# Low halves of the delta branch's chunk matrices: subtraction on GpSimd instead of VectorE

## The chip, the cores and the metric

The kernel is one program on one core of a Trainium2 chip. The metric is the device time of that core in microseconds (us). A core has five engines that run their own instruction queues in order and meet through semaphores: TensorE (PE, matmuls into PSUM), VectorE (DVE), ScalarE (ACT), GpSimd (POOL, which cannot read PSUM) and SyncE (SP, here a queue that only issues DMAs). POOL issues DMAs too.

## What is computed

One inference step of a hybrid backbone for two groups of tokens, 2048 sample tokens and 128 context tokens, with a model width of 1024. After an adaptive RMSNorm, one input projection feeds three branches of width 512, and a gated sum of the branches goes through an output projection:

```python
    proj = jnp.einsum('btd,de->bte', xn, w_in)
    ...
    o_f, s_f = gated_delta_chunked(q, k, v, g[:, :, 0], beta[:, :, 0], s0_f)
    ...
    o_b = chunk_sgu(u_b, v_b, sgu_norm_g, w_spatial, b_spatial) * jax.nn.silu(z_b)
    o_c = fourier_mix(x_c, grid) * jax.nn.silu(z_c)
    ...
    merged = jnp.einsum('btnd,btnd->btd', gt, pb)
    return jnp.einsum('btd,de->bte', merged, w_out), s_f, s_b
```

The change lies in branch A, the gated delta rule, which is run forwards and backwards over the sequence (`dec_strict` and `dec_incl` are masks of decays):

```python
    m = eye + bc[..., :, None] * jnp.einsum('bnhik,bnhjk->bnhij', kc, kc) * dec_strict
    sol = lax.linalg.triangular_solve(m, rhs, left_side=True, lower=True, unit_diagonal=True)
    ...
    qk = jnp.einsum('bnhik,bnhjk->bnhij', qc, kc) * dec_incl
```

## The kernel before

Numbers that need more than 16 bits are kept as a pair of fp16 tiles: the high half is the value rounded to fp16, the low half is what the rounding left. A product of two pairs is three matmuls (`mm3`, L163). Powers of two (`FS` is 4096) bring the values into the range of fp16.

The program is a long stream of matrix products: the normalised tokens (L438 to L469), the q, k, v columns with their short convolution (L606 to L631), branch B (L1155 to L1200), branch C (from L1213) and the merge and output projection. Branch A is cut in 17 chunks of 128 tokens with 4 heads. Its small, dependent steps are written as a Python generator, `delta()` (L1067), and laid between the large products: `pace.tick` (L320), called after each product with an amount of time, moves the generator to its next `yield` for each `QUOTA` of 1.6. So the program order around the change is that of the ticks. The framework then orders each engine's queue by that priority and by a timing model of its own, with the parts under `high_priority` first; what comes out is one fixed order for each engine.

`delta()` runs `prep` (L673) for each chunk and, interleaved with it, `base_inverse` (L758) for the group of chunks before. The groups are chunk 16 alone and then four of four chunks. A scan over all chunks and both directions follows (L917).

`prep` of one chunk, in eight steps:

- transposes of k, v and q on PE (`turned`, L682), squares on ACT (L688), a small addition on DVE (L689) and the power -1/2 on POOL (L690), and the scaled k in `tok` on DVE (L699);
- q split in a pair (L708, L709); `tok` is stored from POOL's queue (L711), transposed on PE (L715) and split into the pair `T` (L716 on ACT, L717 on DVE);
- the product of keys with keys in a PSUM bank (L726). For each direction: four DVE instructions (L731) multiply it by beta and the decays into the fp32 tile `n_` (names n32, three buffers), four ACT copies (L733) take its diagonal blocks into `nd`, ACT makes the high half (L735) and DVE the low half (L736) of `n16` (three buffers), and `late` (L666) queues its store on SP, which is issued at the next call of `late`;
- POOL issues two DMAs of `nd` (L740), from which `base_inverse` starts: its DVE copy L772 waits for them;
- the product of keys with queries (L743). For each direction DVE multiplies it by the decays (L746), ACT makes the high half (L748), DVE the low half (L749), and the store is queued.

The PSUM banks of `prep` come from three pools in turn. In the trace the tiles `n_`, `n16` and `p16` all appear as `n`, `tok` as `tok`, the banks as `b`.

`base_inverse` inverts the 32x32 diagonal blocks, one column after another, by pairs of DVE instructions on SBUF tiles (L779, L780), and splits the result (L785 on ACT, L786 on DVE).

Also on these engines in that stretch: the conversion of weights into pairs (`converting`, L198: ACT L209 and L218, DVE L183 to L187 and L219), and branch B's and C's gate units: ACT L1109 and DVE L1111 evict a bank, POOL multiplies (L1121), ACT squares (L1122), POOL issues the store (L1123).

`beta` carries a factor of 1/FS² through `prep` (L512), which cancels that of the pair products, and is multiplied by FS before the scan (L1092).

Of the kernel before, what the change touches and what calls it, by code (L numbers as in the profile page):

```python
# [14 lines left out]
AF = mybir.ActivationFunctionType  # L15
ALU = mybir.AluOpType
# [21 lines left out]
FS = 4096.0  # L38
# [73 lines left out]
def hybrid_flow_kernel(ctx: ExitStack, tc: tile.TileContext, x_prompt, x_sample, state_delta, c, c_ctx, ln_g, w_ada,  # L112
# [3 lines left out]
    V, A, G, PE, SY = nc.vector, nc.scalar, nc.gpsimd, nc.tensor, nc.sync  # L116
# [9 lines left out]
    def sb(pl, shape, tag, dt=F32, bufs=None):  # L126
        kw = {} if bufs is None else {"bufs": bufs}
        return pl.tile(list(shape), dt, tag=tag, name=nm(tag), **kw)
# [11 lines left out]
    def bank(pl, shape, tag="b"):  # L140
        if pl is ps_d:
            rot[0] += 1
            pl = ps_d[rot[0] % 3]
        return pl.tile(list(shape), F32, tag=tag, name=nm(tag))
# [247 lines left out]
    for blk in range(8):  # L392
# [3 lines left out]
        ps = bank(ps_d, [2, 256])  # L396
# [41 lines left out]
    for ti, (t0, tn) in enumerate(TBS):  # L438
# [13 lines left out]
        for k in range(KT):  # L452
            ps = bank(ps_d, [P, tn])
# [6 lines left out]
        for g in range(4):  # L460
            ps = bank(ps_d if tn == P and g % 2 else ps_mm, [P, tn])
# [12 lines left out]
    def h3(ap):  # L474
        return ap.rearrange("p (h x) -> p h x", h=H)
# [5 lines left out]
    beta, eg, egl, ed, neg = [sb(dp, dsh, n_) for n_ in ("beta", "eg", "egl", "ed", "neg")]  # L481
# [13 lines left out]
    def decays():  # L495
# [13 lines left out]
        pbv = pbs.rearrange("p c (s d h) -> p s d c h", s=2, d=2)  # L509
        for d in range(2):  # L510
            A.activation(beta[:, d], pbv[:, 0, d], AF.Sigmoid, scale=bdw.inv)
        V.tensor_scalar(beta, beta, 1.0 / (FS * FS), None, ALU.mult)  # L512
        yield 1
        NH = 2 * NCH * H
        blob = sb(dq, [P, 2, WB], "tok").rearrange("p d x -> p (d x)")
# [90 lines left out]
    for ct in range(12):  # L606
        w = getw(1, 2 if ct < 6 else min(4, 15 - ct))
        for half in range(1):
# [4 lines left out]
            for t0, tn in TBS:  # L613
                flip[0] ^= 1
                ps = bank(ps_d if flip[0] else ps_mm, [P, tn])
# [50 lines left out]
    def late(dst, src):  # L666

        if owed:
            SY.dma_start(*owed.pop())
        if dst is not None:  # L670
            owed.append((dst, src))

    def prep(g, ci, t, nxt, held):  # L673
# [5 lines left out]
        def turned(part):  # L679
            ps = bank(ps_d, [P, WB])  # L680
            for h in range(H):
                PE.transpose(ps[:, hs(h)], cur[part][:, h, :], ident)  # L682
            return ps
# [13 lines left out]
        ps = turned(1)  # L697
# [15 lines left out]
        ps = bank(ps_d, [P, WB])  # L713
# [8 lines left out]
        dc = cur["dc"]  # L722
        ps = bank(ps_d, [P, WB])
# [3 lines left out]
        nd = sb(d2, [P, 2, H, 32], "nd", bufs=2)  # L727
        for d in range(2):
            n_ = sb(d2, [P, WB], "n32", bufs=3)
            for h in range(H):  # L730
                V.scalar_tensor_tensor(n_[:, hs(h)], ps[:, hs(h)], beta[:, d, t, h:h + 1], dc[:, d, hs(h)], ALU.mult, ALU.mult)  # L731
            for B in range(4):
                A.copy(nd[32 * B:32 * B + 32, d], h3(n_)[32 * B:32 * B + 32, :, 32 * B:32 * B + 32])  # L733
            n16 = sb(d2, [P, 2, WB], "n16", F16, bufs=3)
            A.activation(n16[:, 0, :], n_, AF.Copy, scale=FS)  # L735
            V.scalar_tensor_tensor(n16[:, 1, :], n_, FS, n16[:, 0, :], ALU.mult, ALU.subtract)  # L736
            late(nD[d][t], n16)
            yield 1
        for d in range(2):
            G.dma_start(ndD[g][d, ci].rearrange("h p i -> p h i"), nd[:, d])  # L740
        ps = bank(ps_d, [P, WB])
        for h in range(H):
            mm3(ps[:, hs(h)], pair(T, h), pair(Q16, h))  # L743
        for d in range(2):
            q_ = sb(d2, [P, WB], "n32", bufs=3)
            V.tensor_mul(q_, ps, dc[:, d, :])  # L746
            p16 = sb(d2, [P, 2, WB], "n16", F16, bufs=3)
            A.activation(p16[:, 0, :], q_, AF.Copy, scale=1.0 / FS)  # L748
            V.scalar_tensor_tensor(p16[:, 1, :], q_, 1.0 / FS, p16[:, 0, :], ALU.mult, ALU.subtract)  # L749
            late(qkD[d][t], p16)  # L750
            yield 1

# [314 lines left out]
    def delta():  # L1067
        nonlocal dq
        seq = [(g, ci, t) for g, ts in enumerate(GROUPS) for ci, t in enumerate(ts)]
        held = {1: rows(1, 16), 2: rows(2, 16), 0: rows(0, 16), "dc": decay_rows(16)}  # L1070
        yield from bounds()
        base = iter(())
        for i_, (g, ci, t) in enumerate(seq):
            if ci == 0 and g:
                for r_ in base:
                    if r_:
                        yield 1
                base = base_inverse(g - 1)
            for n_, _ in enumerate(prep(g, ci, t, seq[i_ + 1][2] if i_ < 16 else None, held)):
                yield 1  # L1080
                if next(base, 0):
                    yield 1
        late(None, None)
        for r_ in base:
            if r_:
                yield 1
        for _ in base_inverse(4):
            yield 1
        dl.close()
        dq = pool(dl, "dqb", 1, side="right")  # L1090
        V.tensor_scalar(rq, rq, bnds[:, 2:3], None, ALU.mult)
        V.tensor_scalar(beta, beta, FS, None, ALU.mult)  # L1092
        for d in range(2):
            V.tensor_tensor(eg[:, d], eg[:, d], rq, ALU.mult)
        pace.quota, pace.fine = SCAN, True
        yield from scan()
        dl.close()
        dps.close()
# [35 lines left out]
    ps = bank(ps_x, [P, 4, P])  # L1134
# [20 lines left out]
    for t in range(NCH):  # L1155
        ps = bank(ps_mm, [P, 4, P])
# [30 lines left out]
    for g in range(4):  # L1187
# [5 lines left out]
        for ti, (t0, tn) in enumerate(TBS):  # L1193
            st = vrow[:, t0:t0 + tn]
            ps = bank(ps_mm, [P, tn])
# [17 lines left out]
    for g in range(4):  # L1213
        xw, zw = getw(2, 2)
        for gh in range(1):
# [18 lines left out]
            for q in range(0, NCH, 4):  # L1234
                qn = min(4, NCH - q)
                ps = bank(ps_mm, [P, qn, P])
# [44 lines left out]
            for q4 in range(5):  # L1281
# [8 lines left out]
                if q4 == 2:  # L1290
                    ps = bank(ps_x, [P, P])
# [180 lines left out]
    for i_, t in enumerate(order):  # L1472
# [7 lines left out]
        for i in range(2):  # L1480
            cs = slice(i * 512, (i + 1) * 512)
            ps = bank(ps_mm, [P, 512])
# [45 lines left out]
```

## Time and profile before

| | |
|---|---|
| runs | 2203.88, 2207.9 and 2209.03 us, median 2207.9 us |
| the profiled execution, its own time | 2208.47 us |
| its span, first to last instruction | 2206.7 us |
| mean granted TensorE clock | 0.994 of full speed |
| VectorE busy over the span | 1299.4 us (59%) |
| GpSimd busy over the span | 708.8 us (32%) |
| HBM traffic | 362 MB, 164 GB/s over the span |

All numbers come from one profiled execution. Busy time counts arithmetic and, for the DMA rows of POOL and SP, the issue of a DMA. A group row names the line, the engine, the operation and the tiles (out<-in) with their partitions and elements, then the count, busy us and mean ns, and after the last bar the time for which the engine stood idle in front of these instructions, with what ended it. "issue" means that the profile shows nothing that was waited for. `(+n forms)` says that other sizes are in the same row.

### The profile page before, as it was taken

The page shows a single profiled execution, that of the slowest core. Times are in us where ns is not written, and L with a number is a line of the kernel's source. Part 1 is how long each engine was busy: PE and PEld are TensorE (multiplying, and loading weights), DVE is VectorE, ACT ScalarE, POOL GpSimd, SP SyncE. Part 2 cuts the span into 40 slices and gives each one's busy share as a digit, 9 for nine tenths or more (in the row PEclk, how much of TensorE's full clock was granted, in tenths as well). Part 3 has the DMA queues.
Part 4 walks back from the last instruction along what each step waited for, and adds up shares of the span by engine and source line. Part 5 has one row for each costly group of instructions (what it writes and reads, how often), then busy time and mean ns, then how long its engine had stood idle before and what let it go on. Part 6 is the DMA issues. An engine that isn't in the chain of part 4 may idle for free.

```text
span 2206.7 us, 42033 instructions
## 1 busy us (share of the span) xinstructions
PE 2138.4 (97%) x15966; PEld 1230.7 (56%) x15966; DVE 1299.4 (59%) x3081; ACT 1005.0 (46%) x2322; POOL 708.8 (32%) x860
## 2 busy tenths in 40 slices
PE   7999999999999999899899999899999999999998
PEld 3564444455555588778555565555555444444443
DVE  5736854479869688255665555755574544233454
ACT  3545644455465564344644445655553422222332
POOL 1421333223334322432322223354442222112543
PEclk9999999999999999999999999999999999999999
DMA  8434733277686762433655556766664544333542
GB/s 280 144 94 157 277 98 101 66 214 224 219 245 221 204 187 86 118 116 119 214 178 162 171 158 187 239 185 213 201 204 150 168 124 129 118 101 120 174 149 104
DMA packets 304276, 365.05 MB, mean 165 GB/s; under 512 B 39393, under 2 KB 215626, under 8 KB 302026
## 3 DMA queue, kind: packets, MB, share of 16 engines
q1 hardware_dynamic: 288938, 302.19, 45.3%
q0 software_dynamic: 12688, 51.27, 6.5%
q10 hardware_dynamic: 2448, 8.91, 1.0%
q8 instruction: 125, 2.05, 0.4%
q14 instruction: 77, 0.63, 0.1%
HBM read 234.67 MB, written 127.62 MB: 164 GB/s over the span
## 4 chain that ended last, share of the span: by engine, by line
PE 50%; DMA 6%; DVE 5%; ACT 3%; issue 2%; POOL 1%; SPq 0%; DVEq 0%; POOLq 0%; ACTq 0%
PE b L161 49%; DMA st<-br 1%; DMA wst<-in_w_branch_dram 1%; DVE XB L779 1%; DVE E L780 1%; DMA wst<-in_w_in_dram 1%; DMA XB<-nd 0%; DMA mt<-mrg 0%; ACT of L1032 0%; POOL o L1029 0%; DVE big L1322 0%; DMA mrow<-mrg 0%; DVE wlo L219 0%; ACT big L1321 0%; DMA S<-in_state_delta_dram 0%
## 5 line engine op out<-in xcount | busy, mean ns | idle before, releaser
L161 PE MATMUL b<-xh,whi 128*128 128x512 f16 (+1 forms) x1920 | 651.3, 348 | 4.8 <-DVE vrow L1198 1.7
L161 PE MATMUL b<-xl,whi 128*128 128x512 f16 (+1 forms) x1920 | 652.1, 348 | 0.0
L161 PE MATMUL b<-xh,wlo 128*128 128x512 f16 (+1 forms) x1920 | 651.1, 348 | 0.0
L161 PEld LDWEIGHTS <-whi 128*128 128x128 f16 x3904 | 356.5, 98 | 332.9 <-issue 12.9
L161 PEld LDWEIGHTS <-wlo 128*128 128x128 f16 x1952 | 191.2, 98 | 178.4 <-issue 2.1
L161 PE MATMUL b<-big,bhi 128*128 128x512 f16 (+1 forms) x960 | 250.7, 348 | 1.0 <-DVE big L1322 1.0
L1361 POOL TENSOR_TENSOR mrow<-mrow,sg 128x512 f32<-128x512 f32 (+1 forms) x80 | 94.3, 1179 | 292.9 <-DVE sg L1360 163.8
L161 PE MATMUL b<-big,blo 128*128 128x512 f16 (+1 forms) x480 | 163.3, 347 | 0.0
L1351 ACT ACTIVATE sg<-b,winv 128x512 f32<-128x512 f32 (+1 forms) x120 | 74.1, 618 | 152.2 <-PE b L161 151.8
L161 PEld LDWEIGHTS <-xh 128*128 128x128 f16 x1496 | 117.1, 98 | 29.7 <-issue 1.4
L628 POOL TENSOR_TENSOR cy<-cy,raw 128x545 f32<-128x545 f32 (+1 forms) x48 | 69.8, 1480 | 185.9 <-ACT raw L627 185.9
L161 PEld LDWEIGHTS <-bhi 128*128 128x128 f16 x960 | 87.0, 98 | 75.8 <-issue 0.3
L175 DVE CAST wscb<-wss 128x1 bf16<-128x1 f32 x93 | 14.3, 154 | 186.1 <-ACT wlo L209 84.1
L1360 DVE SCALAR_TENSOR_TENSOR sg<-b,binv,sg 128x512 f32<-128x512 f32 (+1 forms) x80 | 53.5, 668 | 104.5 <-PE b L161 91.3
L848 POOL COPY T<-ES 32x256 f16<-32x256 f16 x68 | 29.4, 432 | 223.0 <-DMA ES<-ei 204.9
L161 PE MATMUL b<-wohi,mh 128*128 128x512 f16 x240 | 91.0, 379 | 2.6 <-ACT mh L1428 2.6
L161 PE MATMUL b<-whi,xl 128*128 128x128 f16 x544 | 92.9, 219 | 0.0
L161 PE MATMUL b<-wlo,xh 128*128 128x128 f16 x544 | 92.9, 219 | 0.0
L161 PE MATMUL b<-whi,xh 128*128 128x128 f16 x544 | 92.9, 219 | 0.0
L219 DVE SCALAR_TENSOR_TENSOR wlo<-wst,wsc,whi 128x1024 f16<-128x1024 f32 x52 | 74.4, 1434 | 28.5 <-ACT whi L218 28.2
L161 PE MATMUL b<-wohi,ml 128*128 128x512 f16 x240 | 90.9, 379 | 0.3 <-DVE mscb L175 0.3
L161 PE MATMUL b<-wolo,mh 128*128 128x512 f16 x240 | 91.0, 379 | 0.0
(449 smaller groups left out, 4283.1 us busy)
## 6 DMA issues: line engine op xcount, KB each, us to landing
wst<-in_w_in_dram SPq DMA_DIRECT2D x60, 512.0 KB, 5.4
qkv<-cy POOLq DMA_DIRECT2D x12, 1089.0 KB, 5.2
st<-br SPq DMA_DIRECT2D x48, 256.0 KB, 5.1
mrow<-mrg SPq DMA_DIRECT2D x18, 512.0 KB, 4.1
mrow<-mrg SPq DMA_DIRECT2D x16, 576.0 KB, 4.4
mrg<-mrow POOLq DMA_DIRECT2D x16, 576.0 KB, 3.6
dc<-dec SPq DMA_DIRECT2D x17, 512.0 KB, 5.2
kq<-qkv SPq DMA_DIRECT2D x34, 256.0 KB, 5.5
```

The costliest lines, as they stand in the source:

```text
L161: PE.matmul(out, l, r, start=start, stop=stop)
L175: V.tensor_copy(sb16, ss)
L219: V.scalar_tensor_tensor(w.lo, st, s, w.hi, ALU.mult, ALU.subtract)
L628: G.tensor_tensor(y[:, c0:c1], y[:, c0:c1], raw[:, 1 + c0:1 + c1], ALU.mult)
L779: V.tensor_tensor(t3, X3[:, 0:k, k:k + 1].to_broadcast([P, k, n_]), E3[:, k:k + 1, k:32].to_broadcast([P, k, n_]), ALU.mult)
L780: V.tensor_tensor(E3[:, 0:k, k:32], E3[:, 0:k, k:32], t3, ALU.subtract)
L848: G.tensor_copy(T16[rows(a0, b), :, :, b], ES[0:32, :, 2 * a0 + b, :, wT])
L1351: A.activation(sg, ps, AF.Sigmoid, scale=gw.inv)
L1360: V.scalar_tensor_tensor(sg, ps, binv[:, 1:2], sg, ALU.mult, ALU.mult)
L1361: G.tensor_tensor(mr, mr, sg, ALU.add)
```

## The change

In `prep`, both low halves (L736, L749) become plain subtractions on GpSimd, fp32 tile minus its fp16 high half. For that the fp32 tile must already have the scale of the pair. For the key product, `beta` now has a factor of 1/FS instead of 1/FS², and the diagonal blocks are divided by FS as they are copied. For the query product, the multiplication by the decays takes 1/FS with it. The high halves become plain copies on ScalarE. The factor that `beta` got before the scan (L1092) goes.

```diff
-        V.tensor_scalar(beta, beta, 1.0 / (FS * FS), None, ALU.mult)
+        V.tensor_scalar(beta, beta, 1.0 / FS, None, ALU.mult)
...
-                A.copy(nd[32 * B:32 * B + 32, d], h3(n_)[32 * B:32 * B + 32, :, 32 * B:32 * B + 32])
+                A.activation(nd[32 * B:32 * B + 32, d], h3(n_)[32 * B:32 * B + 32, :, 32 * B:32 * B + 32], AF.Copy, scale=1.0 / FS)
             n16 = sb(d2, [P, 2, WB], "n16", F16, bufs=3)
-            A.activation(n16[:, 0, :], n_, AF.Copy, scale=FS)
-            V.scalar_tensor_tensor(n16[:, 1, :], n_, FS, n16[:, 0, :], ALU.mult, ALU.subtract)
+            A.copy(n16[:, 0, :], n_)
+            G.tensor_tensor(n16[:, 1, :], n_, n16[:, 0, :], ALU.subtract)
             late(nD[d][t], n16)
...
-            V.tensor_mul(q_, ps, dc[:, d, :])
+            V.scalar_tensor_tensor(q_, ps, 1.0 / FS, dc[:, d, :], ALU.mult, ALU.mult)
             p16 = sb(d2, [P, 2, WB], "n16", F16, bufs=3)
-            A.activation(p16[:, 0, :], q_, AF.Copy, scale=1.0 / FS)
-            V.scalar_tensor_tensor(p16[:, 1, :], q_, 1.0 / FS, p16[:, 0, :], ALU.mult, ALU.subtract)
+            A.copy(p16[:, 0, :], q_)
+            G.tensor_tensor(p16[:, 1, :], q_, p16[:, 0, :], ALU.subtract)
             late(qkD[d][t], p16)
...
-        V.tensor_scalar(beta, beta, FS, None, ALU.mult)
```

## The prediction

> **What bounds the kernel now.** I read the page's first lines first, then the busy time of the stage in which the change lies, then TensorE's waits there, then the groups of VectorE, GpSimd and ScalarE.
>
> ```profile
> span 2206.7 us, 42033 instructions
> PE 2138.4 (97%) x15966; PEld 1230.7 (56%) x15966; DVE 1299.4 (59%) x3081; ACT 1005.0 (46%) x2322; POOL 708.8 (32%) x860
> ```
>
> TensorE (PE) is busy for 97% of the span. No edit here takes a matmul away, so the change can only move the idle time of PE: 68 us in all. The chunk preparation runs from about 440 us to 890 us. The row of the windows view for that stretch gives, after its bounds and length, the busy us (and instructions) of PE, PE's weight loads, VectorE (DVE), ScalarE (ACT) and GpSimd (POOL), then the granted clock.
>
> ```profile
> 440.00:890.00 450.00, 435.33 (x3356) 277.89 (x3355) 365.31 (x957) 242.80 (x722) 142.29 (x180) 0.99 0.66 199
> ```
>
> PE is idle for 14.7 us in these 450, and that is the whole gain that the stage has to give. DVE, at 81%, is the fullest engine beside PE; POOL stands at 32%. The waits of PE in the same stretch (line that waited, what it waited for: us in total, times, longest) say whose the idle time is:
>
> ```profile
> PE b L715 <- DVE tok L699: 2.9, 2, 2.2
> PE b L682 <- issue: 2.6, 1, 2.6
> PE b L161 <- ACT T L716: 2.6, 2, 2.4
> PE b L161 <- DVE vrow L1198: 1.7, 1, 1.7
> PE b L161 <- DVE wsc L185: 1.5, 1, 1.5
> PE b L161 <- DVE T L717: 1.1, 3, 0.4
> PE b L682 <- DVE n L731: 0.8, 2, 0.4
> ```
>
> No wait is long. A dozen small ones make up the sum, each where an instruction of the preparation stands at the head of PE's queue and its input is not there yet.
>
> **The change part by part.** The two subtractions leave DVE. Their groups in the stretch, with neighbours that are needed below (columns: count, busy us, mean ns, idle before and its cause):
>
> ```profile
> L779 DVE TENSOR_TENSOR XB<-XB,E 128x31 f32<-128x31 f32 (+15 forms) x155 | 57.2, 369 | 2.9
> L780 DVE TENSOR_TENSOR E<-E,XB 128x31 f32<-128x31 f32 (+15 forms) x155 | 52.9, 341 | 3.0
> ...
> L749 DVE SCALAR_TENSOR_TENSOR n<-n,n 128x512 f16<-128x512 f32 x34 | 24.5, 726 | 6.9 <-ACT n L748 6.8
> L736 DVE SCALAR_TENSOR_TENSOR n<-n,n 128x512 f16<-128x512 f32 x34 | 23.4, 689 | 7.9 <-ACT n L735 7.8
> L746 DVE TENSOR_TENSOR n<-b,dc 128x512 f32<-128x512 f32 x34 | 22.7, 685 | 1.4 <-PE b L161 1.4
> ...
> L689 DVE TENSOR_SCALAR ss<-ss 128x4 f32<-128x4 f32 x34 | 8.7, 255 | 1.1 <-ACT sq L688 1.0
> ...
> L772 DVE COPY XB<-XB 64x1024 f32<-64x1024 f32 x5 | 5.3, 1059 | 13.4 <-DMA XB<-nd 13.4
> ```
>
> *Removed from DVE:* 24.5 + 23.4 = 47.9 us of work, and 6.8 + 7.8 = 14.6 us in which DVE's queue stood still for ACT's high half: 62.5 us. Where it shows on PE is seen once, at 609.5 us, in the timelines of DVE and PE (start, us, instruction):
>
> ```profile
> 607.26 0.69 DVE L736 SCALAR_TENSOR_TENSOR n<-n,n 128x512 f16<-128x512 f32 x1 [0.28 <-ACT n L735]
> ...
> 608.12 0.69 DVE L749 SCALAR_TENSOR_TENSOR n<-n,n 128x512 f16<-128x512 f32 x1
> 608.73 0.69 DVE L746 TENSOR_TENSOR n<-b,dc 128x512 f32<-128x512 f32 x1
> ```
>
> ```profile
> 609.51 0.66 PE L682 MATMUL b<-cst,qr 128*128 128x128 f32 x4 [2.65 <-issue]
> ```
>
> PE's transposes need a bank that L746 still reads. Ahead of L746 stood one L736, its wait and one L749: 1.7 us. This wait (2.6), those on T L717 (1.1) and n L731 (0.8), and by my choice half of that on tok (1.45) are in reach of a shorter DVE queue: **6.0 us**. Not in reach are T L716 (ACT), vrow (DVE had been waiting for a DMA) and wsc L185 (DVE stood at L772).
>
> *Added to POOL:* 68 subtractions of a 128x512 tile. The same operation stands elsewhere in the program (min/median/max ns):
>
> ```profile
> L957 POOL TENSOR_TENSOR kn<-skn,kn x34: 1145/1157/1663, 903.8 to 1648.7; 128x512 f16<-128x512 f32 x34
> ```
>
> 68 x 1.157 = 78.7 us, so POOL goes from 142 to 221 us of 450: room enough in sum. But POOL is no free neighbour of DVE, as 758 us shows:
>
> ```profile
> 758.82 1.26 POOL L1121 TENSOR_TENSOR st<-sg,vrow 128x512 f32<-128x512 f32 x1 [11.65 <-DVE sg L1111]
> 760.05 1.04 POOL L690 TENSOR_TENSOR ss<-ss,mhalf 128x4 f32<-128x4 f32 x1
> ```
>
> ```profile
> 758.89 1.27 DVE L779 TENSOR_TENSOR XB<-XB,E 128x60 f32<-128x60 f32 x1
> 760.20 0.22 DVE L780 TENSOR_TENSOR E<-E,XB 128x60 f32<-128x60 f32 x1
> 760.46 0.25 DVE L779 TENSOR_TENSOR XB<-XB,E 128x87 f32<-128x87 f32 x1
> ```
>
> A 60-column L779 takes 1.27 us where its twin L780 of the same size takes 0.22: it ends when POOL's 512-column product ends. Under L690, which reads four columns, L779 has its usual length. So a wide POOL instruction holds back a DVE instruction that reads two SBUF tiles. PE waited soon after:
>
> ```profile
> 762.69 0.63 PE L715 MATMUL b<-cst,tok 128*128 128x128 f32 x4 [2.19 <-DVE tok L699]
> ```
>
> How much of it there is now follows from the groups above, the spread of L689 (min/median/max ns) and the wide POOL instructions of the stretch:
>
> ```profile
> L689 DVE TENSOR_SCALAR ss<-ss x34: 155/167/1261, 455.4 to 829.1; 128x4 f32<-128x4 f32 x34
> ```
>
> ```profile
> L1121 POOL TENSOR_TENSOR st<-sg,vrow 128x512 f32<-128x512 f32 (+1 forms) x20 | 23.0, 1151 | 66.6 <-DVE sg L1111 59.8 <-DVE vrow L1198 3.2 <-DVE winv L216 2.0
> ...
> L1121 POOL TENSOR_TENSOR st<-sg,yT 128x512 f32<-128x512 f32 (+1 forms) x5 | 5.5, 1115 | 2.3 <-DVE yT L1274 1.4 <-DVE n L749 0.6 <-DMA br<-st 0.3
> ```
>
> Against what the instructions take undisturbed, L779 lost (over L780, the same shapes) 57.2 - 52.9 = 4.3 us; L749 (over L736) 24.5 - 23.4 = 1.1; L689, with a mean of 255 ns against a median of 167, 34 x 0.088 = 3.0: together 8.4 us. L1121 took 23.0 + 5.5 = 28.5 us, so 8.4 / 28.5 = 0.29 us of DVE is lost for each us of it. The subtractions would cost 78.7 x 0.29 = 23 us (bounds: nothing, and all 78.7). I take 23, which is made of the nearest rows.
>
> The Trainium skill states the reason in "SBUF — State Buffer", section "Who interferes with whom": a VectorE instruction with two SBUF inputs contends with a GpSimd instruction that reads SBUF, and the one that comes second is blocked to the end of the other. The 1.27 us above agree. By that rule at its full length, each of the 68 subtractions with a two-input instruction behind it, all 78.7 us come back on DVE, more than the 62.5 that leave it; this is the third rival below.
>
> Net on DVE: 62.5 - 23 = 39.5 us, 63% of what is removed. Of the 6.0 us of PE in reach I take 63%: **3.8 us gained**.
>
> *ACT.* High halves lose their scale, the nd copies gain one:
>
> ```profile
> L733 ACT COPY nd<-n 32x128 f32<-32x128 f32 x136 | 39.8, 293 | 23.5 <-DVE n L731 22.3
> ...
> L748 ACT ACTIVATE n<-n 128x512 f16<-128x512 f32 x34 | 21.0, 622 | 14.0 <-DMA n<-n 11.5 <-DVE n L749 0.9 <-ACT q L708 0.8
> ```
>
> ```profile
> L956 ACT CAST kn<-skn x34: 600/618/620, 901.7 to 1647.8; 128x512 f16<-128x512 f32 x34
> ```
>
> Scaled 622, plain 618: 4 ns, times 136 copies and 68 halves, under 1 us either way, hidden since ACT is busy 243 of 450 us. ACT also waits 11.5 us for stores of n16 (three buffers). The store now follows a subtraction that is 1.157 - 0.689 = 0.47 longer; 34 times that is 16 us of ACT at most, which I cost at nothing in ACT's idle 207 us; if that cover failed it would be part of the second rival. SP's stores wait the same 0.47 at its queue's head, one step after the data is made; weights are read two ahead. L746 becomes a scaled form: 685 against the 689 of L736, no change. The beta line that goes is a single small instruction.
>
> *New waits on POOL's queue.* Each subtraction waits at the head of the queue for ACT's high half. Behind it stand the DMAs of nd (L740), the power L690, L1121 and the store of kv. Two of them matter.
>
> The second DMA of nd comes after the second subtraction in the program: ACT's conversion (0.62) and the subtraction (1.16) go ahead of it, 1.8 us. DVE's copy L772 waits at its queue's head for that data, 13.4 us over 5 groups, behind which PE lost the 1.5 us of wsc L185. 5 x 1.8 = 9 us more, at 1.5 / 13.4, is **1.0 us lost** (bounds: nothing if the DMA is put first; 9 us if PE loses every one).
>
> L690 releases tok L699, which releases PE's L715. Its slack is small. Around 494 us:
>
> ```profile
> 493.13 1.36 POOL L690 TENSOR_TENSOR ss<-ss,mhalf 128x4 f32<-128x4 f32 x1
> ```
>
> ```profile
> 495.02 0.69 DVE L749 SCALAR_TENSOR_TENSOR n<-n,n 128x512 f16<-128x512 f32 x1
> 495.63 0.69 DVE L746 TENSOR_TENSOR n<-b,dc 128x512 f32<-128x512 f32 x1
> 496.23 0.68 DVE L699 TENSOR_TENSOR tok<-b,ss 128x512 f32<-128x512 f32 x1
> ```
>
> The power is done at 494.49, tok starts at 496.23: 1.7 us in DVE's queue, of which 0.69 is an L749 that goes. A subtraction ahead of L690 makes it 1.16 later, which this slack covers. I take one full subtraction over all 17 chunks: **1.2 us lost** (bounds: nothing, and 17 x 1.16 = 19.7).
>
> **Sum:** -3.8 + 1.0 + 1.2 = -1.6 us. The profiled execution took 2208.47 us, 1.8 more than its span, and 0.6 more than the median of the runs (2207.9). 2208.5 - 1.6 = 2206.9; I forecast **2207**, no difference within 0.3% (6.6 us), which is about what a measurement of this kernel can tell from no change.
>
> **The rivals.** *First, the relief is whole (0.30).* DVE's blocking falls into its own idle time, all 6.0 us in reach go, and the other 1.45 of tok. Then the stall at the scan's start shrinks too (PE's waits from 890 to 1000 us):
>
> ```profile
> PE b L161 <- DVE X L1257: 4.2, 1, 4.2
> ```
>
> DVE stands there behind the scan's first loads, which follow the last base inverse; the last chunk's two L749 (0.7 each) before that inverse are gone, 1.4 us. 6.0 + 1.45 + 1.4 = 8.9: 2200, and 2194 if vrow, wsc and T L716 go as well. For it: DVE's 81%. Against it: the 1.27 us above.
>
> *Second, POOL's in-order queue (0.28), the case on the other side.* L690 stands behind a subtraction that itself waits for ACT, in most chunks, and PE's L715 pays. It decides once 9 or more of the 17 chunks pay a full 1.16: 10.4 - 3.8 + 1.0 = +7.6, 2216; all 17 give +16.9, 2225. I name 2219. For it: PE already waits there (2.9 us). Against it: the slack at 494.
>
> *Third, blocking at full length (0.08).* DVE gets back 78.7 - 62.5 = 16 us more than it lost, so nothing of the 6.0 is gained. PE's 2.2 us at L715 followed the block at 758, 2.2 of 8.4: 16 x 0.26 = 4.2, and 1.0 + 1.2: +6.4, 2215, on the bound.
>
> That the change does not do what it says leaves no case of its own: 68 instructions do change engine; only POOL's reading could be stretched instead of DVE's, which is the second rival.
>
> **How the numbers follow.** Forecast 0.34, rivals 0.30, 0.28 and 0.08. The third is halved over the bound: faster 0.30, same 0.38, slower 0.32. The forecast's own range is 2202 to 2213. For 8 in 10 the range takes in all of the first rival down to 2194 and the second up to 2222, with the rest outside.
>
> **What would show it.** Right: DVE's busy time in this stretch falls by 25 to 45 us, L779's mean rises above L780's by more than the 28 ns of now, POOL rises by 80 us or more, PE's wait for issue before L682 goes, and PE's idle time in the stretch stays within 5 us of 14.7. Wrong: PE's waits on tok L699 grow past 8 us (second rival), DVE's busy time does not fall (third), or PE's idle time falls under 8 us (first). If the time moves by more than the idle time of this stretch does, the order of the scan behind it has changed, which nothing here prices.

## The result, and the profile after

The changed kernel takes 2236.2 us (median of four runs, 2234.1 to 2239.4) against 2205.9 us (2203.1 to 2209.0) for the kernel before, run beside it. The ratio is 1.0138, with a 95% interval of 1.0118 to 1.0159: **1.4% slower, 30 us**, where no difference was forecast. The profiled execution took 2239.4 us and its span is 2237.7, which is 31.0 more than before. These are the first lines of its page:

```profile
span 2237.7 us, 42044 instructions
PE 2147.5 (96%) x15966; PEld 1236.2 (55%) x15966; DVE 1304.6 (58%) x3012; ACT 1007.0 (45%) x2322; POOL 784.8 (35%) x928
```

PE runs the same 15966 matmuls. It was idle for 2206.7 - 2138.4 = 68.3 us and is now idle for 2237.7 - 2147.5 = 90.2 us: 21.9 of the 31.0 are idle time. The other 9.1 are busy time: the same matmuls took longer, at a lower clock (see the end). POOL gained its 68 instructions. **DVE, which has 69 instructions fewer (the 68 and the scaling of `beta`), is busy for 5 us more than before.** That one number says that something went wrong on DVE and not only on POOL.

In the row of the chunk preparation (440 to 890 us, columns as in the prediction):

```profile
440.00:890.00 450.00, 419.06 (x3209) 267.37 (x3207) 354.91 (x843) 236.43 (x707) 215.38 (x248) 0.98 0.64 196
```

PE is idle for 30.9 us of the 450, against 14.7. DVE's 843 instructions take 354.9 us (421 ns each); before, 957 took 365.3 (382 ns). They are fewer by more than 69 because the preparation now reaches further beyond 890 us. The last high half of a query product starts at 867.4 us on ACT, before at 844.5: 22.9 of the 31 us are lost by there. The first matmul of the output projection comes 30.0 later than before (2051.2 against 2021.2), so some 7 more go in the scan and the merge, and 1 at the end.

PE's longest waits in the same stretch:

```profile
PE b L682 <- issue: 11.2, 6, 4.9
PE b L715 <- DVE tok L699: 6.1, 5, 2.7
PE b L161 <- DVE sg L1172: 4.5, 4, 2.6
PE b L161 <- DVE T L717: 4.3, 4, 1.9
```

The wait for issue before L682, which the shorter queue should have removed, went from 2.6 to 11.2 us. T L717 went from 1.1 to 4.3, tok from 2.9 to 6.1, and sg L1172 is new. All are instructions of DVE. Its groups (440 to 920 us, so that the stretch holds as many instructions as the prediction's rows do) say what happened to it:

```profile
L780 DVE TENSOR_TENSOR E<-E,XB 128x31 f32<-128x31 f32 (+15 forms) x155 | 72.9, 470 | 3.5
L779 DVE TENSOR_TENSOR XB<-XB,E 128x31 f32<-128x31 f32 (+15 forms) x155 | 65.2, 421 | 3.0
...
L709 DVE SCALAR_TENSOR_TENSOR q<-qr,qsc,q 128x512 f16<-128x512 f32 x17 | 19.7, 1158 | 3.3 <-ACT q L708 3.1
...
L689 DVE TENSOR_SCALAR ss<-ss 128x4 f32<-128x4 f32 x34 | 14.9, 437 | 8.2 <-ACT sq L688 8.2
...
L1172 DVE TENSOR_SCALAR sg<-sg,vss 128x512 f32<-128x512 f32 x17 | 10.9, 641 | 2.5 <-POOL vss L171 2.1
...
L772 DVE COPY XB<-XB 64x1024 f32<-64x1024 f32 x5 | 6.3, 1266 | 10.9 <-DMA XB<-nd 10.9
```

Two of these groups were not shown of the kernel before:

```profile
L709 DVE SCALAR_TENSOR_TENSOR q<-qr,qsc,q 128x512 f16<-128x512 f32 x17 | 12.7, 746 | 3.1 <-ACT q L708 3.1
...
L1173 DVE TENSOR_SCALAR sg<-sg,vss 128x512 f32<-128x512 f32 x17 | 8.2, 485 | 2.1 <-POOL vss L171 2.0
```

The same instructions, as many of them, on the same shapes, take longer: L780 +20.0 us, L779 +8.0, L709 +7.0, L689 +6.2, the scaling of `sg` +2.7, L772 +1.0. That is 44.9 us come back of the 47.9 removed. All of them read SBUF only. L689, the scaling of `sg` and L772, 9.9 us of the sum, read one wide tile from SBUF and not two. (L216, L219 and L786, 0.9 us each, are left out here and below.) A count over single instructions agrees: from 440 to 940 us DVE's instructions take 61.0 us more than the fast tenth of their like in these runs, against 14.2 before, and 46.0 of the 61.0 fall on instructions whose longest overlap on POOL is with a subtraction. L731, L746, L699 and L717, which read a PSUM bank, have kept their durations (L746 683 ns, before 685).

How such a microsecond reaches PE is seen at 617 us, in the timelines of DVE, POOL and PE:

```profile
617.51 0.25 DVE L780 TENSOR_TENSOR E<-E,XB 128x87 f32<-128x87 f32 x1
617.80 2.67 DVE L779 TENSOR_TENSOR XB<-XB,E 128x60 f32<-128x60 f32 x1
620.40 0.68 DVE L746 SCALAR_TENSOR_TENSOR n<-b,dc 128x512 f32<-128x512 f32 x1
621.00 0.20 DVE L780 TENSOR_TENSOR E<-E,XB 128x60 f32<-128x60 f32 x1
```

```profile
617.32 0.77 POOL L740 DMA_DIRECT2D nd<-nd  x1
618.12 1.16 POOL L736 TENSOR_TENSOR n<-n,n 128x512 f16<-128x512 f32 x1
619.23 1.16 POOL L749 TENSOR_TENSOR n<-n,n 128x512 f16<-128x512 f32 x1
```

```profile
621.18 0.72 PE L682 MATMUL b<-cst,qr 128*128 128x128 f32 x4 [4.94 <-issue]
```

A 60-column L779 takes 2.67 us where its twin L780 takes 0.20. Two subtractions run one behind the other on POOL, from 618.12 to 620.39, and L779 ends just after the second. (Why it wasn't done by 618.0, before the first, the trace doesn't say; POOL was issuing a DMA then.) L746 stands behind it in DVE's queue and frees the bank that PE's transposes want: PE stands for 4.94 us. This is the prediction's own stall at 609 us over again, with a held L779 where an L749 used to stand, and nearly twice as long.

### The profile page after: what moved, and what is told of

It reads as the page before. It is cut to its first block, busy times and chain, and to the rows that moved or that the text cites. A ratio compares the mean times of both kernels' runs of the same rounds, so it can differ in the third digit from the quotient of the medians.

```text
span 2237.7 us, 42044 instructions
## 1 busy us (share of the span) xinstructions
PE 2147.5 (96%) x15966; PEld 1236.2 (55%) x15966; DVE 1304.6 (58%) x3012; ACT 1007.0 (45%) x2322; POOL 784.8 (35%) x928
## 4 chain that ended last, share of the span: by engine, by line
PE 48%; DVE 10%; DMA 8%; ACT 3%; issue 3%; POOL 1%; SPq 1%; DVEq 0%; POOLq 0%; ACTq 0%
PE b L161 47%; DVE E L780 2%; DVE XB L779 2%; DMA st<-br 2%; DMA wst<-in_w_in_dram 1%; DMA mrg<-mrow 1%; DVE wlo L219 1%; DMA XB<-nd 1%; DMA wst<-in_w_branch_dram 1%; DMA ES<-ei 1%; DVE big L1321 1%; DVE n L731 0%; DMA br<-o 0%; DVE q L709 0%; ACT of L1032 0%
## 5 line engine op out<-in xcount | busy, mean ns | idle before, releaser
L628 POOL TENSOR_TENSOR cy<-cy,raw 128x545 f32<-128x545 f32 (+1 forms) x48 | 74.3, 1575 | 184.3 <-ACT raw L627 184.3
L1359 DVE SCALAR_TENSOR_TENSOR sg<-b,binv,sg 128x512 f32<-128x512 f32 (+1 forms) x80 | 53.5, 668 | 106.0 <-PE b L161 90.2
L219 DVE SCALAR_TENSOR_TENSOR wlo<-wst,wsc,whi 128x1024 f16<-128x1024 f32 x52 | 75.3, 1451 | 31.9 <-ACT whi L218 31.7
```

The costliest lines, as they stand in the source:

```text
L219: V.scalar_tensor_tensor(w.lo, st, s, w.hi, ALU.mult, ALU.subtract)
L628: G.tensor_tensor(y[:, c0:c1], y[:, c0:c1], raw[:, 1 + c0:1 + c1], ALU.mult)
L1359: V.scalar_tensor_tensor(sg, ps, binv[:, 1:2], sg, ALU.mult, ALU.mult)
```

## The experiments

Three theories were put against each other. **Theory 1, the port:** a wide POOL instruction that reads SBUF holds DVE instructions that read two tiles from SBUF (the 9.9 us on one-tile instructions lie outside it). **Theory 2, POOL's queue:** the instructions behind the subtractions on POOL (DMAs, the power L690) come too late. **Theory 3, the order:** the edit gave the framework other costs and it laid all queues out anew; the loss is an accident of that order. The order is never held fixed: compared in the traces by the names of the tiles, 913 of PE's 15966 matmuls stand at another place in the changed kernel than in the kernel before, and 436 to 1818 in those variants below that have as many matmuls. Ratios are those to the kernel before, run on the same chip.

### The same edit with the subtractions left on VectorE

Against the changed kernel:

```diff
-            G.tensor_tensor(n16[:, 1, :], n_, n16[:, 0, :], ALU.subtract)
+            V.tensor_tensor(n16[:, 1, :], n_, n16[:, 0, :], ALU.subtract)
...
-            G.tensor_tensor(p16[:, 1, :], q_, p16[:, 0, :], ALU.subtract)
+            V.tensor_tensor(p16[:, 1, :], q_, p16[:, 0, :], ALU.subtract)
```

> The scales are moved as in the change, but both low halves stay on VectorE, as plain subtractions of two SBUF tiles. Theory 1 (SBUF reading: a wide GpSimd subtraction holds back VectorE instructions with two SBUF inputs) and theory 2 (GpSimd's in-order queue: the power behind tok and the nd DMAs stand behind the subtractions) both expect the time of before, 2200 to 2213 us, and L779 and L780 at before's 369 and 341 ns. Theory 3 (the fixed order that the framework writes out came out worse, whatever engine subtracts) expects it clearly slower, 2220 us or more, since the edit reorders the queues too.

2209.3 us, ratio 1.0008 (0.9997 to 1.0019). The row of the preparation:

```profile
440.00:890.00 450.00, 434.68 (x3364) 279.67 (x3363) 365.27 (x956) 244.11 (x722) 142.35 (x180) 1.00 0.67 199
```

It is that of the kernel before to within 1 us on PE, DVE and POOL. The moved scale, on ACT and in `beta`, costs nothing; the loss comes with the engine of the subtraction. Of the variants this one's order is the nearest to that of before (436 matmuls elsewhere), so it says little on theory 3.

### One subtraction at a time

The key product's low half alone on POOL, the query product's on DVE:

```diff
-            G.tensor_tensor(p16[:, 1, :], q_, p16[:, 0, :], ALU.subtract)
+            V.tensor_tensor(p16[:, 1, :], q_, p16[:, 0, :], ALU.subtract)
```

> The change with only the key product's low half on GpSimd; the query product's stays on VectorE as a plain subtraction. Half of the wide reads: theory 1 expects about half of the VectorE time that is held (some 24 of 48 us) and half of the loss, 2214 to 2228 us. Theory 2 expects nearly the whole loss, since this subtraction is the one ahead of the nd DMAs: 2226 us or more. Theory 3 gives no number but no order either.

And the other way round:

```diff
-            G.tensor_tensor(n16[:, 1, :], n_, n16[:, 0, :], ALU.subtract)
+            V.tensor_tensor(n16[:, 1, :], n_, n16[:, 0, :], ALU.subtract)
```

> The change with only the query product's low half on GpSimd, the key's on VectorE as a plain subtraction: the other half of the wide reads, and none of them ahead of the nd DMAs. Theory 1 (SBUF reading) expects what the key half alone showed, held VectorE time about 24 us and 2214 to 2228 us, so that the two halves add up to about the 30 us of the change. Theory 2 (GpSimd's queue) expects before's time within 0.3%, since the nd DMAs do not wait for it.

The key product's alone costs 0.57% (0.38 to 0.76; 2220.2 us), the query product's alone 0.47% (0.31 to 0.63; 2216.8 us). Together that is 1.04 of the 1.38%: each edit has its share, and the second costs more beside the first. VectorE's groups of the two kernels, the first with the key product's on POOL:

```profile
L780 DVE TENSOR_TENSOR E<-E,XB 128x31 f32<-128x31 f32 (+15 forms) x155 | 62.4, 403 | 3.1
...
L749 DVE TENSOR_TENSOR n<-n,n 128x512 f16<-128x512 f32 x34 | 29.2, 858 | 13.3 <-ACT n L748 13.3
```

```profile
L780 DVE TENSOR_TENSOR E<-E,XB 128x31 f32<-128x31 f32 (+15 forms) x155 | 64.2, 414 | 3.2
```

L780's mean, 341 ns before and 470 with both, is about half way with either. A hold can fall on either instruction of a pair, so the sum of L779 and L780 says more: 110.1 us before, 121.8 and 123.1 here, 138.1 with both. In the first the L749 that stayed on DVE is held itself: 858 ns, against 691 for the same plain subtraction with nothing moved to POOL.

### POOL writes as long, but does not read

This tells theory 1 from theory 2. Instead of the subtraction, POOL fills the fp32 tile and the low half with zeros, after the same high half and ahead of the same store. The low halves are zero in it, so a part of the computation is left out.

```diff
-            G.tensor_tensor(n16[:, 1, :], n_, n16[:, 0, :], ALU.subtract)
+            G.memset(n_, 0.0)
+            G.memset(n16[:, 1, :], 0.0)
...
-            G.tensor_tensor(p16[:, 1, :], q_, p16[:, 0, :], ALU.subtract)
+            G.memset(q_, 0.0)
+            G.memset(p16[:, 1, :], 0.0)
```

> The change with each GpSimd subtraction replaced by two GpSimd memsets, of the fp32 tile (which must wait for ScalarE's reads of it, as the subtraction did) and of the low half, so that the low halves are zeros. GpSimd's queue keeps its waits and nearly its time (about 1.0 us for 1.16), but reads no SBUF. Theory 1 expects the loss to go: L780 near 341 ns, time within 6 us of the run without low halves. Theory 2 expects the loss to stay: 2225 us or more, with TensorE's waits on tok L699 as in the change (6 us).

2207.0 us, ratio 1.0004 (0.9992 to 1.0015): nothing lost. The row of the preparation, and groups of DVE (L781 and L782 are L779 and L780 here):

```profile
440.00:890.00 450.00, 434.48 (x3378) 279.86 (x3376) 335.49 (x889) 245.17 (x724) 208.12 (x321) 1.00 0.68 201
```

```profile
L781 DVE TENSOR_TENSOR XB<-XB,E 128x31 f32<-128x31 f32 (+15 forms) x155 | 59.2, 382 | 3.4
L782 DVE TENSOR_TENSOR E<-E,XB 128x31 f32<-128x31 f32 (+15 forms) x155 | 55.7, 359 | 3.4
...
L689 DVE TENSOR_SCALAR ss<-ss 128x4 f32<-128x4 f32 x34 | 18.6, 548 | 7.4 <-ACT sq L688 7.3
```

POOL is busy for 208 us, against 215 with the subtractions, in the same place of the same queue, and it waits there no less (27 us in front of the fills from 440 to 920 us, 19 in front of the subtractions). DVE's pairs have nearly their old durations, and PE is back at 434.5. **Theory 2 falls:** the busy queue alone costs nothing. Theory 3 falls as the main cause too: this kernel's order differs from that of before as much as the change's does (930 matmuls elsewhere, 913 with the change). Nearest to it is the order of the kernel with halved subtractions (below), where 392 matmuls and, by the names, 291 of DVE's 3012 instructions stand elsewhere, and that one loses 1.14%. What an order adds to the holds isn't measured.

### No low halves on any engine

The ceiling of what moving them can bring. The low halves are not computed (the high half is stored in their place), so this part of the computation is left out.

```diff
-            G.tensor_tensor(n16[:, 1, :], n_, n16[:, 0, :], ALU.subtract)
-            late(nD[d][t], n16)
+            late(nD[d][t], n16[:, 0:1, :].to_broadcast([P, 2, WB]))
...
-            G.tensor_tensor(p16[:, 1, :], q_, p16[:, 0, :], ALU.subtract)
-            late(qkD[d][t], p16)
+            late(qkD[d][t], p16[:, 0:1, :].to_broadcast([P, 2, WB]))
```

> The change with the low halves left out: no engine computes them, and the stores write the high half twice (same bytes). It is the ceiling of what taking 47.9 us from VectorE can bring. Theories 1 and 2 expect before or a little better, 2192 to 2206 us, with TensorE idle in the preparation below 14 us and L780 near 341 ns. Theory 3 expects 2220 us or more.

2203.6 us, ratio 0.9987 (0.9974 to 0.9999): with 47.9 us of work gone from DVE and nothing added anywhere, the kernel gains 3 to 5 us (0.13% of 2206 by the ratio, 2208.4 - 2203.6 by the medians). So an engine that took the subtractions over for nothing would bring about as much. PE idles for 15.9 us of the stretch (450 - 434.1), where less than 14 had been expected, and L780 is not at 341 ns (here L778; L777 is L779):

```profile
L778 DVE TENSOR_TENSOR E<-E,XB 128x31 f32<-128x31 f32 (+15 forms) x155 | 59.4, 383 | 3.3
L777 DVE TENSOR_TENSOR XB<-XB,E 128x31 f32<-128x31 f32 (+15 forms) x155 | 52.9, 341 | 3.4
```

The two together take 112.3 us, 2 more than before, with no subtraction anywhere. The mean of one of them can thus move by some 40 ns without the subtractions.

### The kernel before, with POOL reading as well

Nothing is moved. DVE makes the low halves as before, and POOL makes the same subtraction into a spare tile that nobody reads. Against the kernel before:

```diff
+            G.tensor_tensor(sb(d2, [P, WB], "spare", F16), n_, n16[:, 0, :], ALU.subtract)
             late(nD[d][t], n16)
...
+            G.tensor_tensor(sb(d2, [P, WB], "spare", F16), q_, p16[:, 0, :], ALU.subtract)
             late(qkD[d][t], p16)
```

> The kernel before, with all of VectorE's work kept, and 68 GpSimd subtractions of the same tiles added, whose result goes into a spare tile that nobody reads. Theory 1 expects the held time of the change (about 48 us) on top of the 47.9 us that stay: L780 at 430 ns or more, and at least the loss of the change, 2232 us or more; 2245 us would be no surprise. A theory by which the loss came from the low half being ready later (stores, buffers, nd DMAs) expects before's time within 0.5%, 2197 to 2219 us.

2247.0 us, ratio 1.0167 (1.0141 to 1.0192): more than the change itself lost, though no low half is later by POOL's 0.47 and no store waits for POOL. (The tiles come free later, as they do with the zero fills, which cost nothing.) Groups of DVE (L781 and L782 are L779 and L780, L750 is L749):

```profile
L781 DVE TENSOR_TENSOR XB<-XB,E 128x31 f32<-128x31 f32 (+15 forms) x155 | 64.0, 413 | 3.0
L782 DVE TENSOR_TENSOR E<-E,XB 128x31 f32<-128x31 f32 (+15 forms) x155 | 62.5, 403 | 3.0
L750 DVE SCALAR_TENSOR_TENSOR n<-n,n 128x512 f16<-128x512 f32 x34 | 38.3, 1133 | 3.3 <-ACT n L749 3.3
```

The pairs are held less than with the change (413 and 403 ns; 430 or more had been expected), because the low half L750, which follows the same high half as POOL's subtraction does, takes part of the hold: 1133 ns for 726. POOL's reading is enough for the loss, whatever its result is for.

### One SBUF input in place of two

The product `t3` of a base inverse goes to a PSUM bank, so that L780 reads one tile from SBUF and one from PSUM, in the changed kernel and in the kernel before:

```diff
-            t3 = tmp[:, 0:k * n_].rearrange("p (j i) -> p j i", j=k)
+            t3 = bank(ps_x, [P, 256])[:, 0:k * n_].rearrange("p (j i) -> p j i", j=k)
```

The changed kernel with it:

> The change, with the base inverse's product (written by L779, read by L780) in a PSUM bank instead of SBUF. L780 then has one SBUF input, L779 still two. Theory 1 in its full form (two SBUF inputs are what is held) expects no L780 stretched under a wide GpSimd read any more, L779 still stretched, and a part of the loss back, less what PSUM operands add: 2215 to 2232 us. If any VectorE instruction were held by GpSimd's reading, L780 would stay stretched and the time would be 2235 us or more.

The kernel before with it:

> The kernel before with the base inverse's product in PSUM, as in the run above. Theory 1 expects nothing to win: L780 is hardly held in before (341 ns), PSUM operands cost VectorE some 10 us, so 2204 to 2216 us. It is the reference for the run above: the difference between the two is what the moved subtractions cost when L780 cannot be held, which theory 1 expects below 22 us, against 30 us with the product in SBUF.

The changed kernel with it takes 2229.9 us (ratio 1.0092, 1.0061 to 1.0122), the kernel before with it 2222.9 (1.0066, 1.0046 to 1.0085). DVE's groups, first of the changed kernel:

```profile
L779 DVE TENSOR_TENSOR b<-XB,E 128x31 f32<-128x31 f32 (+15 forms) x155 | 76.1, 491 | 2.9
L780 DVE TENSOR_TENSOR E<-E,b 128x31 f32<-128x31 f32 (+15 forms) x155 | 51.9, 335 | 3.4
...
L709 DVE SCALAR_TENSOR_TENSOR q<-qr,qsc,q 128x512 f16<-128x512 f32 x17 | 23.4, 1379 | 3.4 <-ACT q L708 3.2
```

```profile
L779 DVE TENSOR_TENSOR b<-XB,E 128x31 f32<-128x31 f32 (+15 forms) x155 | 57.4, 370 | 2.7
L780 DVE TENSOR_TENSOR E<-E,b 128x31 f32<-128x31 f32 (+15 forms) x155 | 51.9, 335 | 3.0
```

This is the sharpest test of theory 1: L780 with one SBUF input takes 335 ns beside the subtractions and 335 without them. It is not held. L779, which still has two, and L709 meet the holds instead. As a cure it fails: the kernel before loses 0.66% by this edit alone, beyond the 2204 to 2216 us that had been expected, presumably since the bank is taken from PE. The 10 us that PSUM operands were to cost DVE did not come (370 and 335 ns, before 369 and 341). That the two then lie only 7 us apart fits the theory but doesn't measure it: 31.3 us are still held (L779 18.7, L709 10.7, the others 1.9), and PE's waits for banks may cover them.

### Halving the length of a hold

Each subtraction of the changed kernel is cut into two of 256 columns, so that DVE could get in between:

```diff
-            G.tensor_tensor(n16[:, 1, :], n_, n16[:, 0, :], ALU.subtract)
+            for c in (slice(0, 256), slice(256, 512)):
+                G.tensor_tensor(n16[:, 1, c], n_[:, c], n16[:, 0, c], ALU.subtract)
```

> The change with each subtraction cut into two of 256 columns. The same bytes are read by GpSimd, in pieces of half the length. If the length of one hold is what hurts, the loss falls to about half, 2212 to 2226 us. If it is the sum of GpSimd's reading time, it stays at 2230 us or more, since two short subtractions take longer than one.

2231.8 us, ratio 1.0114 (1.0083 to 1.0145): at best a small part comes back; the interval overlaps that of the change. The pieces cost POOL more in sum (47.3 + 49.4 = 96.7 us against 80.7 for whole ones), L780 still takes 448 ns, and PE is busy for 419.1 us of the stretch, as with the change. The holds did not get half as long: the longest L780 takes 3.07 us, with the change 3.24, more than two pieces at 0.75 us each. One hold can outlast the end of a piece, as with the two subtractions at 618 us, so what holds of half the length would cost stays open.

### Is it the amount of VectorE work?

The kernel before with L779 computed twice, which adds somewhat more DVE work (54.8 us) at the same place than the holds do, but work that the framework knows of when it lays out the queues:

```diff
             V.tensor_tensor(t3, X3[:, 0:k, k:k + 1].to_broadcast([P, k, n_]), E3[:, k:k + 1, k:32].to_broadcast([P, k, n_]), ALU.mult)
+            V.tensor_tensor(t3, X3[:, 0:k, k:k + 1].to_broadcast([P, k, n_]), E3[:, k:k + 1, k:32].to_broadcast([P, k, n_]), ALU.mult)
```

> The kernel before, with the base inverse's product L779 computed twice: some 57 us more VectorE work in the very chain in which the change's held time lies, but as instructions of their own that the framework counts in when it writes out the order. If held time costs so much because it lies in this place of VectorE's queue, this run should lose at least as much as the change, 2232 us or more. If it costs so much because it comes in pieces of up to 1.2 us that the written order does not count on, this run should lose little: the low halves on VectorE cost about 5 us per 48 us (with against without them), so 2208 to 2220 us.

2232.4 us, ratio 1.0121 (1.0089 to 1.0153), about as much as the change: by the mark set for it, this speaks for the place. PE's two longest waits in it are not those of the change:

```profile
PE b L715 <- DVE XB L779: 7.3, 1, 7.3
PE b L682 <- DVE winv L216: 6.3, 1, 6.3
```

They end at 786.9 and 689.6 us, in the preparation, and ahead of each DVE had stood at L772 for a DMA:

```profile
687.67 1.03 DVE L772 COPY XB<-XB 64x1024 f32<-64x1024 f32 x1 [8.40 <-DMA n<-n]
784.92 1.03 DVE L772 COPY XB<-XB 64x1024 f32<-64x1024 f32 x1 [7.70 <-DMA XB<-nd]
```

The last high half of a query product starts at 857.8 us, 13.3 later than before, which is about what these two waits make. The other half of the loss comes behind it, where the last base inverse, doubled too, ends at 930.9 us against 876.8. So an L772 that comes too early in DVE's queue, a longer last inverse and the load itself are mixed here, and the run settles nothing alone. The next kernel leaves that one alone, and starts from the kernel whose POOL only writes (the low halves are zero in it too):

```diff
-                V.tensor_tensor(t3, X3[:, 0:k, k:k + 1].to_broadcast([P, k, n_]), E3[:, k:k + 1, k:32].to_broadcast([P, k, n_]), ALU.mult)
+            for _ in range(2 if g < 4 else 1):
+                V.tensor_tensor(t3, X3[:, 0:k, k:k + 1].to_broadcast([P, k, n_]), E3[:, k:k + 1, k:32].to_broadcast([P, k, n_]), ALU.mult)
```

> The run with memsets (no GpSimd read, low halves zero), with the product L779 computed twice in the four base inverses that run beside the preparation: some 46 us of VectorE work, about what the change's reads held, in the same chain, but as instructions that the framework counts in; the last base inverse, which runs alone, is left as it is. VectorE's load then equals that of before and of the change. If the place in VectorE's queue is what makes held time dear, this run loses 20 us or more against the run with memsets (2227 us or more). If it is that the held pieces are not in the written order, it loses about as little as the low halves cost on VectorE, 3 to 10 us (2210 to 2217 us).

2211.1 us, ratio 1.0011 (1.0002 to 1.0021). The row of the preparation and the doubled group (L782 is L779 here):

```profile
440.00:890.00 450.00, 430.86 (x3354) 276.95 (x3352) 366.05 (x1012) 243.30 (x722) 203.65 (x317) 1.00 0.67 199
```

```profile
L782 DVE TENSOR_TENSOR XB<-XB,E 128x31 f32<-128x31 f32 (+15 forms) x279 | 99.3, 356 | 6.0
```

99.3 - 59.2 = 40 us more of DVE work than in the kernel it starts from cost some 4 us (2211.1 against 2207.0; by the ratios 1.5). DVE is then busy for 366 us of the stretch, 11 more than with the change, and PE for 430.9 against 419.1. So **at the load of the kernel before, neither DVE's work nor the place is what is dear.** Work in the written order costs about 0.1 us or less for each us of DVE up to that load; with the change, at about the same load, a hold costs several times that (below). It is no rule for any load: on top of all the work of before, the doubled products that ran before the last high half (123 x 368 ns = 45 us) went with 13.3 us, 0.3 us per us, the two waits behind L772 included.

### Without the low halves altogether

As a bound: the low halves are neither computed nor stored, loaded or multiplied, so a part of the computation is left out.

```diff
-            G.tensor_tensor(n16[:, 1, :], n_, n16[:, 0, :], ALU.subtract)
-            late(nD[d][t], n16)
+            late(nD[d][t][:, 0, :], n16[:, 0, :])
...
-            mm3(ps[:, hs(h)], pair(qk_, h), pair(u, h))
+            mm2(ps[:, hs(h)], qk_[:, 0, hs(h)], pair(u, h))
```

> The change with the two low halves left out everywhere: neither computed, stored, loaded nor multiplied, so that the masked key and query products enter the base levels and the output as single fp16 tiles. That is less computation than the reference's numbers get in the other kernels, so its time stands beside the others as a bound only. No held time (as in the run with memsets) and 272 small matmuls fewer, at some 0.06 us each about 16 us: every theory expects it faster than before, 2180 to 2198 us.

2180.8 us, ratio 0.9887 (0.9856 to 0.9917), with 272 matmuls fewer. What the low halves cost is their matmuls and loads, 1.1%, and hardly their making (0.13%, above). None of the kernels that compute everything is measurably faster than the one before.

## Why the prediction was wrong

**The kind of loss was right, its size wrong, and so was the likeliest case.** The time, 2236, lies beyond the range's 2222 and beyond the third rival's 2215.

- *Removed from DVE, 62.5 us.* The 47.9 us of work went. Of the waiting, a part only changed its place: before L689 DVE waits 8.2 us for ACT (1.0 before), and before L746 2.4 us for POOL, whose row is below.
- *"The change can only move the idle time of PE."* 21.9 of the 31.0 us are idle time; the other 9.1 are the same matmuls at a lower clock, for which the sum has no term.
- *PE's 6.0 us in reach.* About right as a ceiling: without the work, on no engine, the kernel gains 3 to 5 us.
- *Added to POOL, 78.7 us, and its price to DVE of 23.* Here are POOL's groups and DVE's L746 (440 to 920 us):

```profile
L749 POOL TENSOR_TENSOR n<-n,n 128x512 f16<-128x512 f32 x34 | 40.5, 1194 | 18.6 <-ACT n L748 18.5
L736 POOL TENSOR_TENSOR n<-n,n 128x512 f16<-128x512 f32 x34 | 40.2, 1182 | 0.7
```

```profile
L746 DVE SCALAR_TENSOR_TENSOR n<-b,dc 128x512 f32<-128x512 f32 x34 | 22.9, 683 | 4.9 <-PE b L161 2.5 <-POOL n L736 2.4
```

  The 80.7 us were nearly right. The rate was not: 44.9 / 80.7 = **0.56 us of DVE held for each us of POOL, against 0.29**. The 0.29 was taken from L1121's neighbours and left out L709, L1173 and L772; and a subtraction perhaps meets the pairs of L779 and L780 more often than L1121 does (not counted).
- *The step that failed* is "Net on DVE: 62.5 - 23 = 39.5 us, 63% of what is removed", and the 3.8 us of PE made from it. In work it is 47.9 - 44.9 = 3 us. But with no relief at all the sum would have come to +2.2 us, not +30. The second half of the step failed too: it let PE follow DVE's sum in proportion, and so did the third rival (16 us at 0.26). PE doesn't pay for the sum. It pays where a hold stands ahead of an instruction it needs now: 4.94 us at one place.
- *What a held us costs,* reckoned as above in the groups of each kernel: with the key product's on POOL 28.4 us were held (L780 9.5, L689 6.5, L749 5.9 over a plain subtraction, L709 3.5, L779 2.2, `sg` 0.8) and 12.9 of span lost; with the query product's 17.6 (L780 11.3, L779 1.7, L772 1.4, L709 1.3, the others 1.9) and 8.6; with both 44.9 and 31.0; in the kernel before with reads added 42.0 (L749 13.8, L780 9.6, L779 6.8, L736 4.8, L709 3.8, the others 3.2) and 39.3. That is 0.45, 0.49, 0.69 and 0.94 us per us. With the product in PSUM, where 31.3 us more are held in the changed kernel, it is 7.0 / 31.3 = 0.2. Against these stand 0.1 or less for work in the order up to the load of before, and 0.3 for work on top of it, which is what the reads added to the kernel before must be set against. It isn't a constant: what was taken off DVE is in the first three, nothing in the fourth. Nor is every hold dear: in the kernel where POOL only writes, L689 was held for 9.9 us (18.6 - 8.7) and nothing was lost.
- *Why a hold is dearer than work* is argued, not shown: the framework fixes each queue by a timing model, which counts an instruction that it lays there and can't count a hold (2.67 - 0.20 = 2.5 us at 617 us) that depends on how DVE and POOL meet in the run. No kernel here kept the order fixed, so how much of the 31 us is the holds and how much a layout that suits them badly stays open.
- *ACT.* Right: L733 went from 293 to 305 ns, 136 times, 1.6 us, and the variant with the subtractions on DVE shows that it costs nothing.
- *The second DMA of nd, 1.0 us lost.* Wrong in sign: L772 waits 10.9 us for it, before 13.4.
- *L690 behind a subtraction, 1.2 us, and the second rival.* PE's wait on tok L699 rose by 3.2 us to 6.1, under the mark of 8. In the kernel where POOL only writes the same queue has no such wait worth the name (1.3 us), so even these seem to belong to the holds.
- *The signs asked for.* POOL's rise came out at 73 us in the stretch (80 had been set). L779 and L780 rose by 52 and 129 ns, which was the right place to look, but L779's mean is now 49 ns below L780's and not above it; that L780 would lose most was not foreseen. DVE fell by 10 us, neither the 25 to 45 of the forecast nor the nothing of the third rival; the 3 us of net work are nearer to the latter, since the stretch now ends before the preparation does. The last line of the list held: the time moved by more (31) than the idle time of the stretch did (16).

The rule of the Trainium skill in "SBUF — State Buffer", section "Who interferes with whom", that the prediction set beside the 1.27 us, has held in each test of the pairs: two SBUF inputs held, one not held (335 and 335 ns), a writing POOL little danger to them (359 and 382 ns). As the prediction put it, it doesn't cover the 9.9 us on one-tile instructions. It was read as an upper bound on DVE's time, 78.7 us. By DVE's time 44.9 of it came; by PE's time the bound was too low.

## What to carry to other kernels

Before elementwise work goes from VectorE to GpSimd, list what VectorE will run beside it: if that reads two SBUF tiles, a part of GpSimd's time comes back on VectorE (0.4 to 0.7 us for each us of subtraction in these runs). Price it at PE's stalls, not at VectorE's spare time. To part a port from a queue, let the other engine write for as long without reading; to part a load from its place, add work that the order knows of. And first take the work out altogether: here it would have shown that only 0.1 to 0.2% was to be had.

## What the runs showed of the hardware

*A stall of PE can be paid twice.* PE's clock fell behind some of them. Rows of the changed kernel after the stall that ended at 621.18 (the granted clock is the third number from the end):

```profile
616.00:620.00 4.00, 0.24 (x5) 0.06 (x2) 3.90 (x5) 3.95 (x15) 3.95 (x5) 1.00 0.66 179
620.00:624.00 4.00, 2.82 (x25) 2.77 (x26) 3.33 (x9) 2.54 (x5) 2.44 (x3) 0.70 0.56 163
624.00:628.00 4.00, 4.00 (x18) 1.67 (x16) 3.62 (x3) 4.00 (x12) 2.35 (x4) 0.88 1.06 361
628.00:632.00 4.00, 4.00 (x23) 2.07 (x21) 2.06 (x5) 1.56 (x6) 3.00 (x7) 1.00 0.86 247
```

The clock lost (1 - 0.70) x 4 + (1 - 0.88) x 4 = 1.7 us. In rows of 0.5 us the granted clock reads 0.50 to 0.57 from 621.5 to 625.0 us and 1.00 around it: half speed for about 3.4 us. The kernel before shows the same behind its stall of 2.19 us at 762.7:

```profile
760.00:764.00 4.00, 1.81 (x10) 0.83 (x9) 3.69 (x14) 1.32 (x3) 3.80 (x6) 0.95 1.05 297
764.00:768.00 4.00, 4.00 (x18) 1.71 (x17) 3.79 (x10) 0.15 (x1) 0.00 (x0) 0.63 0.33 131
```

(1 - 0.95) x 4 + (1 - 0.63) x 4 = 1.7 us again. So a PE stall of some 2 us or more can cost 1.7 us on top. Not each does: none of it followed the stall of 2.36 us at 713.7 in the kernel before. Over the span the mean granted clock is 0.989 with the change and 0.994 before; 0.005 x 2238 = 11 us fits PE's 9.1 us of extra busy time. The Trainium skill, in "TensorE: Matmul & The Clock Gate", section "Part 1: The HAM clock gate", has half rate after an idle window of about 3.4 us, and full rate again after about 3.4 us of sustained work. The length of the slow piece agrees with the second; against the first, a stall of 2.19 us was enough here to bring one.

*A writing GpSimd holds VectorE too, elsewhere.* With the zero fills, L689, a TENSOR_SCALAR from SBUF to SBUF with one tile as its input, went from 255 to 548 ns, and the scaling of `sg`, a TENSOR_SCALAR too, from 485 to 604, while the two-input pairs stayed within 18 ns of before.
